# Sixteen meta queries and one filler product moved inside the first attention of a two-block kernel

## The chip, the cores and the metric

The kernel runs on one core of one Trainium2 chip. The metric is the device time of one execution in microseconds (us); the time before is the median of three runs. TensorE (PE) does the matrix products, VectorE (DVE) and ScalarE (ACT) the elementwise work, SyncE (SP) issues nearly all DMAs. Each engine runs its own instructions in a fixed order and waits on semaphores for the others.

## The reference, cut to what matters

The reference is two transformer blocks behind one another. The first one puts 16 meta tokens ahead of 512 tokens, normalises, projects, and mixes a state-space branch (`y_ssm`) with a differential attention branch. For each of 4 heads and each of 528 queries the attention is

```python
s = q . k                                  # two of them per head, j = 0 and 1
s = s - slope * dist ; s = where(dist >= 0, s, NEG_INF)
p = softmax(s)
w = p[:, :, 0] - lam * p[:, :, 1]
o = w @ v
y_att = rmsnorm(o, subln_g) * (1 - lam_init)
mixed = sigmoid(g_ssm) * (y_ssm @ w_ssm_out) + sigmoid(g_att) * (y_att @ w_att_out)
```

Then come an output product, a gated feed-forward part, and the second block (linear attention, sparse attention and two mixtures of experts). Only the first block's attention is touched by the change. Of the 16 meta queries only the last 2 are needed, for the convolution of the feed-forward part; the keys and values of all 16 are needed.

## The kernel before, in words

All large products are made of three float32 matmuls on split operands (`mm3`, lines 394 to 396: high by high, high by low, low by high). A weight tile is split into its high and low half by an ACT cast and a DVE subtraction (`split`, line 369). `dense_fm` makes one 128-row block of an output out of such matmuls; for 512 features in it issues 4 x 2 x 3 = 24.

The attention goes through 16 tiles, j = 0 to 15: query block i = j // 4 of 128 queries, head h = j % 4. I call them heads 0 to 15. `score` (lines 854 to 876) makes the two score tiles of a head on PE (line 861), adds the distance term (L863), takes the maximum (L867), the exponential on ACT (L869), the reciprocals (L870) and weighs the two halves into one (L874, L875). `weigh` (lines 878 to 895) transposes the weights on PE (L883), copies them back with ACT (L884 to L888), multiplies by the values (L893, tile `pv`), copies the result (DVE, L894) and sums its squares (ACT, L895). The score of head j + 1 is issued ahead of the weights of head j. After the fourth head of a query block `att_out` (lines 838 to 851) normalises: `rsq` (lines 433 to 440) is a chain of eleven small DVE instructions with the first one at L841, each using the result of the one before; then a scaling by row (the next L360), four transposes (L847, tile `yat`), and the high and low half of the result (ACT L850, DVE L851).

So that PE has work while the softmax runs, twelve products of the state-space branch are kept as fillers, in this order: `glu` 0 to 3 (lines 902 to 912) and `ssm_out` 0 to 7 (lines 923 to 928; its gate is read by DMA, L917, and goes through ACT at L918 and DVE at L919 and L920). One of them, 24 matmuls, is issued before `weigh` in each tile with j % 4 not zero:

```python
        nx = score((j + 1) // 4, (j + 1) % 4) if j < 15 else None
        if j % 4:
            filler(1)
        weigh(i, h, w_, osb, ss4)
```

After the 16 tiles stand the 16 meta queries (lines 946 to 982): eight tiny score products, a softmax on 16 partitions (L360, L959 to L965), four transposes, four products with the values, four sums of squares (L981) and an `att_out` of their own. Behind them the product with `w_att_out` begins (lines 988 to 992). Its columns come in two halves of 258 and 256 tokens, and all of `y_att` in a half has to be there for it.

The program is written in this order, but the order of the instructions on each engine is set before the run by a scheduler that looks at dependencies; what it made of the text is shown below where the prediction needs it.

Of the kernel before, what the change touches and what calls it, by code (L numbers as in the profile page):

```python
# [14 lines left out]
AF = mybir.ActivationFunctionType  # L15
ALU = mybir.AluOpType
AX = mybir.AxisListType
PSUM = bass.MemoryType.PSUM

P = 128  # L20
# [8 lines left out]
MID0 = T - MID  # L29
# [239 lines left out]
def build(ctx, tc, I, out, dbg=None):  # L269
    nc = tc.nc  # L270
    V, A, G, TE = nc.vector, nc.scalar, nc.gpsimd, nc.tensor
# [13 lines left out]
    def sb(n, tag, dt=F32, bufs=1):  # L285
        return ar.get(n, tag, dt, bufs)

    def p2(name):
        return pp_.tile([P, 2, 512], F32, tag="p2", name=name, bufs=3)
# [7 lines left out]
    def small(name, shape, dt=F32, bufs=1, tag=None):  # L297
        return sm.tile([P] + list(shape), dt, tag=tag or name, name=name, bufs=bufs)
# [60 lines left out]
    def tt(o, a, b, op, eng=None):  # L359
        return (eng or V).tensor_tensor(o, a, b, op=op)  # L360

    def bc(ap, n):
        return ap.unsqueeze(ap.ndim).to_broadcast(list(ap.shape) + [n])
# [83 lines left out]
    g1, ones, ident = (load_c(n, eng=nc.scalar) for n in ('g1', 'c_ones', 'c_ident'))  # L447
# [4 lines left out]
    with tc.manual_schedule(engines={mybir.EngineType.SP}):  # L452
# [5 lines left out]
        blk, b16 = load_c('c_blk'), load_c('c_b16')  # L458
# [253 lines left out]
    uT, qn = tiles(4, T, "uT"), tiles(4, T, "qn")  # L712
    for m in range(4):
        ps = dense_fm(KD, x1, HC)
# [27 lines left out]
    def filler(n):  # L742
        for _ in range(min(n, len(fill))):
            f, m = fill.pop(0)
            f(m)
# [18 lines left out]
    rq = small("rq", (40,))  # L764
# [21 lines left out]
    for c, (k0, n) in enumerate(kch):  # L786
        V.tensor_scalar(kdst[c], o[c][:n], r1c[:n, c:c + 1], None, op0=ALU.mult)
        s_ = sb(512, "t1", bufs=3)
# [49 lines left out]
    def att_out(osb, ss4, n, t0, skip=0):  # L838

        o4 = osb[:n].rearrange("p (h e) -> p h e", h=4)  # L840
        V.tensor_scalar(ss4[:n], ss4[:n], 1.0 / P, EPS, op0=ALU.mult, op1=ALU.add)  # L841
        r4 = small("r4", (4,), bufs=2)
        rsq(r4, ss4, (4,))
        tt(o4, o4, bc(r4[:n], P), ALU.mult)
        ps = p1("yat")
        for h in range(4):
            TE.transpose(ps[:, h * P:h * P + n], osb[:n, h * P:(h + 1) * P], ident[:n, :n])  # L847
        src = ps.rearrange("p (h t) -> p h t", h=4)[:, :, skip:n]
        hs = yahv[:, :, t0:t0 + n - skip]
        A.activation(hs, src, AF.Identity, scale=sgs)  # L850
        V.scalar_tensor_tensor(yalv[:, :, t0:t0 + n - skip], src, sgs, hs.bitcast(F32), op0=ALU.mult, op1=ALU.subtract)  # L851

    def score(i, h):
        n, q0 = NM + P * (i + 1), NM + P * i
        nb, w = (2, n // 2) if n > 512 else (1, n)
        pj, rj = [], []
        for j in range(2):
            ps = p2("sc")
            rows = slice(64 * j, 64 * j + 64)
            for b_ in range(nb):  # L860
                TE.matmul(ps[:, b_, :w], qn[h][rows, q0:q0 + P], knv[rows, h, b_ * w:(b_ + 1) * w], start=True, stop=True)
            s_ = sb(T, "s", bufs=6)
            V.scalar_tensor_tensor(s_[:, :n].rearrange("p (a b) -> p a b", a=nb), ps[:, :nb, :w],  # L863
                                   rq[:, 8 * (i + 1) + 2 * h + j:8 * (i + 1) + 2 * h + j + 1],
                                   dh[h][:, T - n:].rearrange("p (a b) -> p a b", a=nb), op0=ALU.mult, op1=ALU.add)
            mx = small("mx", (1,), bufs=6)
            V.tensor_reduce(mx, s_[:, :n], axis=AX.X, op=ALU.max, negate=True)  # L867
            se = small("se", (1,), bufs=6)
            A.activation(s_[:, :n], s_[:, :n], AF.Exp, bias=mx, accum_out=se)  # L869
            V.reciprocal(se, se)  # L870
            pj.append(s_)
            rj.append(se)
        tt(rj[1], rj[1], nlam, ALU.mult)
        V.tensor_scalar(pj[1][:, :n], pj[1][:, :n], rj[1], None, op0=ALU.mult)  # L874
        V.scalar_tensor_tensor(pj[0][:, :n], pj[0][:, :n], rj[0], pj[1][:, :n], op0=ALU.mult, op1=ALU.add)  # L875
        return pj[0]
# [53 lines left out]
    glu_b2 = small("glu_b2", (4,))  # L930
    V.tensor_scalar(glu_b2, glu_b, 0.5, None, op0=ALU.mult)
    fill = [(glu, m) for m in range(4)] + [(ssm_out, m) for m in range(8)]
    w_ = score(0, 0)
    for j in range(16):
        i, h = j // 4, j % 4
        if h == 0:
            osb = sb(512, "osb", bufs=2)
            ss4 = small("ss4", (4,), bufs=2)
        nx = score((j + 1) // 4, (j + 1) % 4) if j < 15 else None
        if j % 4:  # L940
            filler(1)
        weigh(i, h, w_, osb, ss4)
        w_ = nx
        if h == 3:
            att_out(osb, ss4, P, 2 + P * i)
    ps = p2("sc16")
    for h in range(4):
        for j in range(2):
            rows = slice(64 * j, 64 * j + 64)
            TE.matmul(ps[:16, j, (h * 16):(h + 1) * 16], qn[h][rows, 0:16], knv[rows, h, 0:16], start=True, stop=True)  # L950
    s_ = sb(256, "s", bufs=6)
    sv = s_[:16, :128].rearrange("p (h j k) -> p h j k", h=4, j=2)
    rq0 = rq[:16, 0:8].rearrange("p (h j) -> p h j", j=2)
    for j in range(2):
        tt(sv[:, :, j], ps[:16, j, :64].rearrange("p (h k) -> p h k", h=4), bc(rq0[:, :, j], 16), ALU.mult)
    s3 = s_[:16, :128].rearrange("p (a k) -> p a k", k=16)
    tt(s_[:16, :128], s_[:16, :128], b16, ALU.add)
    mx = small("mx8", (8,))[:16]
    V.tensor_reduce(mx, s3, axis=AX.X, op=ALU.max)  # L959
    tt(s3, s3, bc(mx, 16), ALU.subtract)  # L960
    A.activation(s_[:16, :128], s_[:16, :128], AF.Exp)
    V.tensor_reduce(mx, s3, axis=AX.X, op=ALU.add)
    V.reciprocal(mx, mx)
    m2 = mx.rearrange("p (h j) -> p h j", j=2)
    V.tensor_scalar(m2[:, :, 1], m2[:, :, 1], nlam[:16], None, op0=ALU.mult)  # L965
    tt(s3, s3, bc(mx, 16), ALU.mult)
    w16 = s_[:16, 128:192]
    tt(w16.rearrange("p (h k) -> p h k", h=4), sv[:, :, 0], sv[:, :, 1], ALU.add)
    ps = p2("w16t")
    for h in range(4):  # L970
        TE.transpose(ps[:16, 0, h * 16:(h + 1) * 16], w16[:, h * 16:(h + 1) * 16], ident[:16, :16])
    w16t = s_[:16, 192:256]
    A.copy(w16t, ps[:16, 0, :64])
    for h in range(4):
        TE.matmul(ps[:16, 1, h * P:(h + 1) * P], w16t[:, h * 16:(h + 1) * 16], vm[:, h * P:(h + 1) * P], start=True, stop=True)
    osb = sb(512, "osb", bufs=2)
    ss4 = small("ss4", (4,), bufs=2)
    V.memset(ss4, 1.0)
    A.copy(osb[:16], ps[:16, 1])
    for h in range(4):  # L980
        A.activation(ps[:16, 0, h * P:(h + 1) * P], osb[:16, h * P:(h + 1) * P], AF.Square, accum_out=ss4[:16, h:h + 1])  # L981
    att_out(osb, ss4, 16, 0, skip=MID0)
    drop_tiles("qn", "dh", "uT", "zh", "zl")
    drop("kn", "vt", "vm", "s", "wT", "osb")
    ya = pairs([yahv[:, h] for h in range(4)], [yalv[:, h] for h in range(4)])
# [29 lines left out]
    ps = p2("rs2")  # L1015
# [997 lines left out]
```

## Time and profile before

| | |
|---|---|
| median of three runs | 1919.12 us (1915.56 to 1922.62) |
| the profiled execution | 1922.88 us, span of its records 1921.1 us |
| PE busy with matmuls | 1749.1 us (91%), 10719 instructions |
| DVE busy | 1219.8 us (63%) |
| ACT busy | 877.3 us (46%) |
| mean granted TensorE clock | 0.948 of full speed |

Times of the trace count from the start of the span. The first attention with its fillers lies between about 255 and 374 us. "Busy" of PE is the time in which some matmul is in its pipeline. An idle time in brackets stands before the instruction that ended it, with the instruction that released it behind the arrow. SBUF tiles are cut from pages and are all called `pg`; PSUM tiles keep their names (`sc`, `wtp`, `pv`, `yat`, `mm`).

### The profile page before, as it was taken

How to read it: one execution, taken by the hardware profiler on the slowest of the kernel's cores; microseconds unless marked ns; L12 is line 12 of the kernel's file. 1: busy time of each engine (PE TensorE's matmuls, PEld its weight loads, DVE VectorE, ACT ScalarE, POOL GpSimd, SP SyncE). 2: the span in 40 equal slices, each digit the busy share in tenths (PEclk: the TensorE clock that was granted, in tenths of full speed). 3: DMA queues.
4: the chain of work that ended last, by engine and by line, in shares of the span. 5: the costliest groups of instructions: out<-in, count | busy, mean ns of one | idle time of the engine just before them, and what ended most of it. 6: DMA issues, size and time to landing. Idle time of an engine off the chain costs nothing.

```text
span 1921.1 us, 27208 instructions
## 1 busy us (share of the span) xinstructions
PE 1749.1 (91%) x10719; PEld 1484.6 (77%) x10719; DVE 1219.8 (63%) x2276; ACT 877.3 (46%) x1397; POOL 168.2 (9%) x140
## 2 busy tenths in 40 slices
PE   8999999899999999999999699949998999869990
PEld 7899877798989988877888578838786777648870
DVE  7755368776555543235347879874437777678985
ACT  4233346433333332234213278854235675638881
POOL 2310000022000000000000112110000000012213
PEclk9999999899999999999989899979899999979995
DMA  5435222242222233222215589762131003548953
GB/s 194 111 109 139 89 88 65 64 158 96 103 89 88 92 140 106 94 88 88 88 67 203 185 292 382 300 230 77 58 140 45 1 12 111 203 156 327 382 216 140
DMA packets 69206, 269.73 MB, mean 140 GB/s; under 512 B 22144, under 2 KB 24721, under 8 KB 44241
## 3 DMA queue, kind: packets, MB, share of 16 engines
q1 hardware_dynamic: 52384, 246.38, 36.0%
q0 software_dynamic: 9216, 16.80, 2.3%
q10 hardware_dynamic: 7472, 4.76, 1.2%
q8 instruction: 85, 1.39, 0.3%
q14 instruction: 49, 0.39, 0.1%
HBM read 249.62 MB, written 30.43 MB: 146 GB/s over the span
## 4 chain that ended last, share of the span: by engine, by line
PE 64%; DVE 6%; ACT 3%; DMA 2%; issue 1%; POOL 0%; POOLq 0%; SPq 0%; DVEq 0%; ACTq 0%
PE mm L396 8%; PE mm L395 8%; PE mm L394 8%; PE psh L395 3%; PE psh L396 3%; PE psh L394 3%; PE tm L395 2%; PE tm L394 2%; PE tm L396 2%; PE npo L1932 2%; PE npt L1920 2%; PE op L395 2%; PE op L394 2%; PE op L396 2%; PE xgt L1436 1%
## 5 line engine op out<-in xcount | busy, mean ns | idle before, releaser
L369 ACT CAST pg<-pg 128x1024 fp32r<-128x1024 f32 (+2 forms) x437 | 428.3, 1003 | 564.3 <-PE mm L395 225.3
L369 DVE TENSOR_TENSOR pg<-pg,pg 128x1024 fp32r<-128x1024 f32 (+2 forms) x437 | 503.3, 1175 | 277.5 <-ACT pg L369 262.6
L396 PE MATMUL mm<-pg,pg 128*128 128x258 f32 (+2 forms) x1504 | 483.3, 322 | 3.9 <-DVE pg L369 3.8
L394 PE MATMUL mm<-pg,pg 128*128 128x258 f32 (+2 forms) x1504 | 485.3, 323 | 1.4 <-ACT pg L888 0.7
L395 PE MATMUL mm<-pg,pg 128*128 128x258 f32 (+2 forms) x1504 | 482.9, 321 | 0.0
L394 PEld LDWEIGHTS mm<-pg,pg 128*128 128x128 f32 x1504 | 288.0, 192 | 27.8 <-ACT pg L886 2.7
L396 PEld LDWEIGHTS mm<-pg,pg 128*128 128x128 f32 x1504 | 287.0, 191 | 25.0 <-DVE pg L369 4.7
L395 PEld LDWEIGHTS mm<-pg,pg 128*128 128x128 f32 x1504 | 287.9, 191 | 21.2 <-issue 0.4
L360 DVE TENSOR_TENSOR pg<-mm,pg 128x256 f32<-128x256 f32 (+3 forms) x138 | 66.3, 510 | 140.2 <-PE mm L396 140.2
L394 PE MATMUL psh<-pg,pg 128*128 128x512 f32 x256 | 106.3, 415 | 7.4 <-ACT pg L369 7.4
L395 PE MATMUL psh<-pg,pg 128*128 128x512 f32 x256 | 106.0, 414 | 1.3 <-DVE pg L369 1.3
L396 PE MATMUL psh<-pg,pg 128*128 128x512 f32 x256 | 104.3, 407 | 0.7 <-DVE pg L369 0.6
L395 PE MATMUL tm<-pg,pg 128*128 128x512 f32 x192 | 76.9, 401 | 2.2 <-DVE pg L369 2.2
L396 PE MATMUL tm<-pg,pg 128*128 128x512 f32 x192 | 76.0, 396 | 0.0
L394 PE MATMUL tm<-pg,pg 128*128 128x512 f32 x192 | 75.5, 403 | 0.0
L360 DVE TENSOR_TENSOR pg<-pg,pg 128x512 f32<-128x512 f32 (+12 forms) x103 | 57.6, 580 | 24.9 <-ACT pg L675 9.3
L1904 ACT ACTIVATE pg<-ns,nmx 128x512 f32<-128x512 f32 (+3 forms) x128 | 66.5, 535 | 11.3 <-DVE nmx L1900 7.2
L394 PEld LDWEIGHTS psh<-pg,pg 128*128 128x128 f32 x256 | 50.2, 196 | 19.0 <-ACT pg L369 8.7
L1900 DVE TENSOR_REDUCE nmx<-ns 128x2 f32<-128x1024 f32 (+3 forms) x48 | 50.0, 1042 | 17.0 <-PE ns L1897 16.8
L360 DVE TENSOR_TENSOR pg<-pg 128x64 f32<-128x64 f32 (+8 forms) x127 | 49.3, 409 | 17.4 <-ACT pg L1033 15.4
L1426 POOL DMA_INDIRECT pg<-xd,idx x32 | 39.5, 1236 | 236.4 <-DVE wts L360 128.0
L395 PEld LDWEIGHTS psh<-pg,pg 128*128 128x128 f32 x256 | 50.2, 196 | 12.9 <-DVE pg L369 2.5
(440 smaller groups left out, 2955.0 us busy)
## 6 DMA issues: line engine op xcount, KB each, us to landing
pg<-in_w_moe_dram SPq DMA_DIRECT2D x96, 1024.0 KB
pg<-in_w_up_dram SPq DMA_DIRECT2D x22, 1024.0 KB
pg<-in_w_dn_dram SPq DMA_DIRECT2D x11, 1024.0 KB
pg<-in_w_g_dram SPq DMA_DIRECT2D x8, 1024.0 KB
pg<-in_w_go_dram SPq DMA_DIRECT2D x8, 1024.0 KB
pg<-yd SPq DMA_DIRECT2D x16, 512.0 KB
pg<-in_w_n_dram SPq DMA_DIRECT2D x8, 1024.0 KB
pg<-in_w_no_dram SPq DMA_DIRECT2D x8, 1024.0 KB
```

The lines of the kernel that those rows point to most:

```text
L360: return (eng or V).tensor_tensor(o, a, b, op=op)
L369: return A.copy(h, src), V.tensor_tensor(l, src, h.bitcast(F32), op=ALU.subtract)
L394: TE.matmul(o, a[0], b[0], start=start, stop=False)
L395: TE.matmul(o, a[0], b[1], start=False, stop=False)
L396: return TE.matmul(o, a[1], b[0], start=False, stop=stop)
L1426: ld = G.indirect_dma_start(out=xg, out_offset=None, in_=self.xd, in_offset=bass.IndirectOffsetOnAxis(ap=self.idx[:, e:e + 1], axis=0), bo ...
L1436: i = TE.transpose(ps[:, k // 4, (k % 4) * P:(k % 4 + 1) * P], xg[:, k * P:(k + 1) * P], ident)
L1900: V.tensor_reduce(mx, sc, axis=AX.X, op=ALU.max, negate=True)
L1904: A.activation(pp[:, r, br], sc[:, r, br], AF.Exp, bias=mx[:, r, br:br + 1], accum_out=se[:, r, br:br + 1])
L1920: TE.transpose(src[:, r, br, c * P:(c + 1) * P], pp[:, r, br, c * P:(c + 1) * P], ident)
L1932: TE.matmul(o_[64 * r:64 * r + 64], vsw[:, c * 512 + br * 256 + g * 64:c * 512 + br * 256 + (g + 1) * 64], pts[r][:, br, c * P:(c + 1) * P ...
```

## The change

The meta queries become a function `meta()`, called after the weights of head 8; its tiles `osb16` and `ss16` are those of `att_out` for it. The filler call of tile j = 1 is dropped; the fillers keep their order, so that each of the first eleven comes in the next tile that has one, and the twelfth is issued after the weights of head 15, ahead of the last `att_out`. No arithmetic changes.

```diff
+    def meta():
+
+        ps = p2("sc16")
...
+        w16 = s_[:16, 128:192]
...
+        osb16 = sb(512, "osb", bufs=2)
+        ss16 = small("ss16", (4,))
+        V.memset(ss16, 1.0)
+        A.copy(osb16[:16], ps[:16, 1])
...
+        att_out(osb16, ss16, 16, 0, skip=MID0)
+
     w_ = score(0, 0)
     for j in range(16):
         i, h = j // 4, j % 4
@@ -937,49 +977,16 @@
             osb = sb(512, "osb", bufs=2)
             ss4 = small("ss4", (4,), bufs=2)
         nx = score((j + 1) // 4, (j + 1) % 4) if j < 15 else None
-        if j % 4:
+        if j % 4 and j > 1:
             filler(1)
         weigh(i, h, w_, osb, ss4)
         w_ = nx
+        if j == 8:
+            meta()
+        if j == 15:
+            filler(1)
         if h == 3:
             att_out(osb, ss4, P, 2 + P * i)
-    ps = p2("sc16")
...
-    att_out(osb, ss4, 16, 0, skip=MID0)
```

What the scheduler makes of it shows at three places. At the start, on PE, around the scores of heads 2 and 3 (`sc`), the transposes of head 1 (`wtp`) and the first filler (`mm`); the rows with + are new here, the filler's first two matmuls follow them:

```order
 L893 MATMUL pv<-pg_243,pg_81 128x128
 L861 MATMUL sc<-pg_80,pg_428 128x144
+L883 MATMUL wtp<-c_ident,pg_132 16x128
+L883 MATMUL wtp<-c_ident,pg_132 128x128
+L861 MATMUL sc<-pg_80,pg_428 128x144 x2
+L893 MATMUL pv<-pg_102,pg_2687 128x128
+L893 MATMUL pv<-pg_243,pg_2687 128x128
 L394 MATMUL mm<-pg_2622,pg_430 128x258
 L395 MATMUL mm<-pg_2623,pg_430 128x258
```

The filler stood behind the second row and now stands behind the value products of head 1.

In the middle, on DVE, ahead of the first score row of head 11 (the L863). Before (a row of the normaliser of query block 1, head 10's weights, then the score):

```order
L440 SCALAR_TENSOR_TENSOR r_3111<-rsqt,r_3111 128x4
L875 SCALAR_TENSOR_TENSOR pg_132<-pg_132,se,pg_81 128x400
L360 TENSOR_TENSOR rsqt<-r_3111 128x4
L863 SCALAR_TENSOR_TENSOR pg_81<-sc,rq,pg_262 128x400
L439 SCALAR_TENSOR_TENSOR rsqt<-rsqt,ss_2889 128x4
```

With the change (`ss_3166` and `r_3174` are the meta queries' sums and factors, `pg_430` a weight tile):

```order
L440 SCALAR_TENSOR_TENSOR r_3174<-rsqt,r_3174 128x4
L360 TENSOR_TENSOR rsqt<-r_3174 128x4
L439 SCALAR_TENSOR_TENSOR rsqt<-rsqt,ss_3166 128x4
L440 SCALAR_TENSOR_TENSOR r_3174<-rsqt,r_3174 128x4
L360 TENSOR_TENSOR pg_2687<-pg_2687,r_3174 16x512
L919 SCALAR_TENSOR_TENSOR pg_3062<-pg_3062,mm 128x258
L920 SCALAR_TENSOR_TENSOR pg_3062<-pg_3062,mm 128x256
L369 TENSOR_TENSOR pg_430<-pg_92,pg_430 128x1024
L863 SCALAR_TENSOR_TENSOR pg_2687<-sc,rq,pg_262 128x400
```

Head 10's weights lie well ahead now, and the whole chain of the meta normaliser, which nothing interleaves, has come in between them and head 11's score.

At the end, on PE, from the last value products (`pv`, here of head 15) to the product with `w_att_out` (`mm<-pg_2620`, `mm<-pg_2621`). Before:

```order
L893 MATMUL pv<-pg_102,pg_2687 128x128
L893 MATMUL pv<-pg_243,pg_2687 128x128 x4
L971 MATMUL w16t<-c_ident,pg_132 16x16 x4
L975 MATMUL w16t<-pg_102,pg_132 16x128 x4
L847 MATMUL yat<-c_ident,pg_2687 128x128 x4
L847 MATMUL yat<-c_ident,pg_132 128x16 x4
L394 MATMUL mm<-pg_2620,pg_430 128x258 x2
```

With the change (the first row is the last matmul of the twelfth filler):

```order
L396 MATMUL mm<-pg_2624,pg_483 128x256
L893 MATMUL pv<-pg_243,pg_2687 128x128 x4
L394 MATMUL mm<-pg_2620,pg_430 128x258
L395 MATMUL mm<-pg_2621,pg_430 128x258
L396 MATMUL mm<-pg_2620,pg_430 128x258
L394 MATMUL mm<-pg_2620,pg_430 128x258
L395 MATMUL mm<-pg_2621,pg_430 128x258
L396 MATMUL mm<-pg_2620,pg_430 128x258
L394 MATMUL mm<-pg_2620,pg_483 128x258
L395 MATMUL mm<-pg_2621,pg_483 128x258
L396 MATMUL mm<-pg_2620,pg_483 128x258
L847 MATMUL yat<-c_ident,pg_132 128x128 x4
```

The meta products are gone from here, and nine matmuls on the first column half of the next product have come ahead of the last transposes.

## Rows read from the trace of the kernel before

**Rows 1.** Stages: us; busy PE, PEld, DVE, ACT, POOL; granted clock, DMA share, GB/s
```profile
274.54:287.90 13.36, 11.83 (x75) 9.24 (x74) 9.13 (x31) 9.65 (x29) 0.00 (x0) 1.00 0.47 159
287.90:315.91 28.01, 26.39 (x163) 19.94 (x163) 25.27 (x77) 17.93 (x57) 0.00 (x0) 1.00 0.16 50
315.91:324.76 8.85, 6.96 (x47) 5.10 (x47) 8.20 (x31) 5.57 (x18) 0.00 (x0) 1.00 0.13 35
324.76:349.24 24.48, 22.20 (x146) 18.79 (x147) 20.40 (x53) 15.68 (x40) 0.00 (x0) 0.93 0.23 71
349.24:374.16 24.92, 18.43 (x152) 15.62 (x152) 19.62 (x68) 12.99 (x41) 0.00 (x0) 0.90 0.30 97
374.16:379.25 5.09, 5.09 (x23) 5.09 (x24) 0.20 (x1) 0.00 (x0) 0.00 (x0) 0.50 0.18 52
344.50:347.40 2.90, 2.90 (x24) 2.90 (x24) 2.90 (x12) 2.31 (x7) 0.00 (x0) 1.00 0.00 0
```

**Rows 2.** Timeline, PE at the end: start us, us, instruction, [idle before, releaser]
```profile
360.75 4.55 PE L893 MATMUL pv<-pg,pg 16*128 16x128 f32 x30 [0.45 <-DVE pg L851]
369.05 1.01 PE L847 MATMUL yat<-c_ident,pg 128*128 128x128 f32 x4 [1.78 <-DVE pg L360]
373.22 0.58 PE L847 MATMUL yat<-c_ident,pg 16*128 16x16 f32 x4 [3.16 <-DVE pg L360]
```

**Rows 3.** Timeline, DVE at the end: meta softmax, normaliser, scaling, low halves
```profile
360.52 0.33 DVE L360 TENSOR_TENSOR pg<-sc,rq 16x64 f32<-16x64 f32 x2
364.60 0.21 DVE L360 TENSOR_TENSOR pg<-pg 16x64 f32<-16x64 f32 x1
366.12 0.17 DVE L841 TENSOR_SCALAR ss<-ss 128x4 f32<-128x4 f32 x1 [0.49 <-ACT pv L895]
368.30 0.69 DVE L360 TENSOR_TENSOR pg<-pg,r 128x512 f32<-128x512 f32 x1
371.35 0.74 DVE L851 SCALAR_TENSOR_TENSOR pg<-yat,sgs,pg 128x512 fp32r<-128x512 f32 x1
374.14 0.23 DVE L851 SCALAR_TENSOR_TENSOR pg<-yat,sgs,pg 128x8 fp32r<-128x8 f32 x1 [1.07 <-ACT pg L850]
```

**Rows 4.** Timeline, ACT at the end: the meta queries' copy, a square, the high half
```profile
367.36 0.58 ACT L979 COPY pg<-w16t 16x512 f32<-16x512 f32 x1 [0.65 <-PE w16t L975]
368.40 0.27 ACT L981 ACTIVATE w16t<-pg 16x128 f32<-16x128 f32 x1
368.62 0.18 ACT L981 ACTIVATION_READ_ACCUMULATOR w16t<-pg 16x1 f32 x1
370.09 0.69 ACT L850 ACTIVATE pg<-yat,sgs 128x512 fp32r<-128x512 f32 x1 [0.43 <-PE yat L847]
```

**Rows 5.** Timeline, start: scores, a gate on ACT, head 1's transposes, a filler's DVE pass
```profile
277.36 0.51 PE L861 MATMUL sc<-pg,pg 64*128 64x144 f32 x2
279.58 0.64 ACT L918 ACTIVATE pg<-pg 128x514 f32<-128x514 f32 x1 [0.86 <-DMA pg<-sgd]
281.42 0.38 PE L883 MATMUL wtp<-c_ident,pg 128*16 128x128 f32 x2 [0.49 <-DVE pg L875]
283.00 0.69 DVE L910 SCALAR_TENSOR_TENSOR pg<-pg,pg 128x514 f32<-128x514 f32 x1
```

**Rows 6.** Timeline, middle, DVE and ACT: a split, a head's two weighing passes, an exponential
```profile
314.41 1.22 DVE L369 TENSOR_TENSOR pg<-pg,pg 128x1024 fp32r<-128x1024 f32 x1
320.99 0.42 DVE L874 TENSOR_SCALAR pg<-pg,se 128x400 f32<-128x400 f32 x1
322.49 0.62 DVE L875 SCALAR_TENSOR_TENSOR pg<-pg,se,pg 128x400 f32<-128x400 f32 x1
327.14 0.61 ACT L869 ACTIVATE pg<-pg,mx 128x400 f32<-128x400 f32 x1
```

**Rows 7.** Timeline, PE: the two longest waits between the start and the last tiles
```profile
323.26 0.60 PE L883 MATMUL wtp<-c_ident,pg 128*16 128x128 f32 x4 [1.62 <-DVE se L360]
349.24 0.70 PE L883 MATMUL wtp<-c_ident,pg 128*16 128x128 f32 x5 [1.62 <-DVE se L870]
```

More of the change, by code (lines that the diff above doesn't have):

```diff
@@ L932, in build @@
     fill = [(glu, m) for m in range(4)] + [(ssm_out, m) for m in range(8)]
+    def meta():
+        ps = p2("sc16")
+        for h in range(4):
+            for j in range(2):
+                rows = slice(64 * j, 64 * j + 64)
+                TE.matmul(ps[:16, j, (h * 16):(h + 1) * 16], qn[h][rows, 0:16], knv[rows, h, 0:16], start=True, stop=True)
+        s_ = sb(256, "s", bufs=6)
+        sv = s_[:16, :128].rearrange("p (h j k) -> p h j k", h=4, j=2)
+        rq0 = rq[:16, 0:8].rearrange("p (h j) -> p h j", j=2)
+        for j in range(2):
+            tt(sv[:, :, j], ps[:16, j, :64].rearrange("p (h k) -> p h k", h=4), bc(rq0[:, :, j], 16), ALU.mult)
+        s3 = s_[:16, :128].rearrange("p (a k) -> p a k", k=16)
+        tt(s_[:16, :128], s_[:16, :128], b16, ALU.add)
+        mx = small("mx8", (8,))[:16]
+        V.tensor_reduce(mx, s3, axis=AX.X, op=ALU.max)
+        tt(s3, s3, bc(mx, 16), ALU.subtract)
+        A.activation(s_[:16, :128], s_[:16, :128], AF.Exp)
+        V.tensor_reduce(mx, s3, axis=AX.X, op=ALU.add)
+        V.reciprocal(mx, mx)
+        m2 = mx.rearrange("p (h j) -> p h j", j=2)
+        V.tensor_scalar(m2[:, :, 1], m2[:, :, 1], nlam[:16], None, op0=ALU.mult)
+        tt(s3, s3, bc(mx, 16), ALU.mult)
+        w16 = s_[:16, 128:192]
+        tt(w16.rearrange("p (h k) -> p h k", h=4), sv[:, :, 0], sv[:, :, 1], ALU.add)
+        ps = p2("w16t")
+        for h in range(4):
+            TE.transpose(ps[:16, 0, h * 16:(h + 1) * 16], w16[:, h * 16:(h + 1) * 16], ident[:16, :16])
+        w16t = s_[:16, 192:256]
+        A.copy(w16t, ps[:16, 0, :64])
+        for h in range(4):
+            TE.matmul(ps[:16, 1, h * P:(h + 1) * P], w16t[:, h * 16:(h + 1) * 16], vm[:, h * P:(h + 1) * P], start=True, stop=True)
+        osb16 = sb(512, "osb", bufs=2)
+        ss16 = small("ss16", (4,))
+        V.memset(ss16, 1.0)
+        A.copy(osb16[:16], ps[:16, 1])
+        for h in range(4):
+            A.activation(ps[:16, 0, h * P:(h + 1) * P], osb16[:16, h * P:(h + 1) * P], AF.Square, accum_out=ss16[:16, h:h + 1])
+        att_out(osb16, ss16, 16, 0, skip=MID0)
     w_ = score(0, 0)
@@ L943, in build @@
         w_ = nx
+        if j == 8:
+            meta()
+        if j == 15:
+            filler(1)
         if h == 3:
             att_out(osb, ss4, P, 2 + P * i)
-    ps = p2("sc16")
[L947 to L981, printed above, removed]
-    att_out(osb, ss4, 16, 0, skip=MID0)
     drop_tiles("qn", "dh", "uT", "zh", "zl")
```

## The prediction

> **What bounds the kernel now.** I read the page first (table above): PE is the busiest engine over the whole span, so a change inside the attention is worth what it does to PE's idle time there, not to any engine's sum. Then I cut the attention into five stages with the view of engines by stretch [rows 1], at instants that can be found again in the changed kernel: the first score row on DVE (L863) of heads 4, 9 and 11, the transposes of head 13's weights (L883), and the first matmul of the product with `w_att_out` behind the last `yat`. I call them A to E; they last 13.36, 28.01, 8.85, 24.48 and 24.92 us. The reader should see that DVE is nearly as full as PE: in stage B 25.27 us of DVE stand beside 26.39 of PE, in stage C 8.20 us of 8.85 are DVE's and only 6.96 are PE's. So the softmax on DVE sets the pace in C, and both engines together in B and D. Only E has room on both (18.43 and 19.62 of 24.92).
>
> Then the timeline of PE at the end [rows 2]: the value products of the last three heads end at 365.30 (360.75 + 4.55), and the next product begins at 374.16. In between PE idles 1.78 us for the normaliser of query block 3, 3.16 us for that of the meta queries, and the clock falls: the stretch after it runs 23 matmuls in 5.09 us at a granted clock of 0.50, where 24 take 2.90 us at 1.00 [rows 1]. That is the lower of the two levels, 1.2 GHz, after some 9 us of scattered small products; it costs 2.3 us. This gap is what the change fills. The question is what it pays elsewhere.
>
> **The change, stage by stage.** The order of each engine (shown with the change) gives what moves; durations are from rows.
>
> *A, the first filler gone.* 24 matmuls (2.90 us) and two DVE passes of 0.69 us [rows 1, 5] leave the stage. PE did not need the room: its queue waited at 281.42 for head 1's weights, which waited for an exponential behind a gate on ACT that came by DMA at 279.58 [rows 5]. This wait stays, now with PE empty from the end of the scores at 277.87 on, 3.5 us [rows 5]. DVE saves 1.37 us of passes, so the stage could end 1.3 us sooner. But the filler now follows the transposes of head 1 and two more scores (281.42 + 0.38 + 2 x 0.51, an estimate of 282.8), and head 2's transposes queue behind it on PE. If the clock has fallen in the gap, the filler loses what the lower level cost stage D, 7% of 24.48 us or 1.7 us [rows 1], and the stage ends by as much later. The 3.5 us without work are more than the 1.62 us before the transposes at 323.26 [rows 7], which ended with that lower clock; so I take the lower level: **+0.4 us**, ends -1.3 and +1.0.
>
> *B, each filler one place later.* PE's load stays. DVE loses a split (1.22) and the two passes of a head's weights (0.42 + 0.62) that fall into C, and gains the two passes from A (1.37) [rows 5, 6]: -0.9 us. PE and DVE share this stage, so I take half: **-0.5**, ends 0 and -0.9.
>
> *C, the meta queries.* DVE has no room, so its queue is what I add up. The meta softmax is ten instructions of 0.2 to 0.3 us, 2.3 us together (first and last in [rows 3]). The meta normaliser is eleven instructions that start 0.20 us apart because each needs the last (366.12 to 368.30 for the same chain), then 0.69 to scale and 0.23 for the low half [rows 3]: 3.1 us, with nothing of another head between them. The scheduler draws other work ahead of head 11's score: the split and a head's weights of above (2.3), and scaling and low half of query block 1 (0.69 + 0.74) [rows 3, 6]: 3.7 us. Waits are new, since head 10 now stands alone: both reciprocals wait for their exponentials (0.61 us, and a read-out as long as that of a square, 0.18) [rows 4, 6] with only one or no DVE instruction to cover them: 0.45 and 1.0 us by hand. Before the meta normaliser ACT has a high half (0.69), the copy (0.58) and five sums of squares (0.45 each) [rows 4], 3.5 us, against 2.4 us of DVE work: 1.1 us. Head 10's score waits 0.3 us for the meta transposes ahead of it on PE. That is 2.85 us of waits, against 0.65 us that DVE idled in C before [rows 1]. Sum: 2.3 + 3.1 + 3.7 + 2.2 = **+11.3 us**, ends +8.5 (no waits) and +12.5. On PE the small meta products lie within this, covered.
>
> *D gives a part back.* Query block 1's scaling and low half (1.43) have left DVE. PE, fuller here (22.20 of 24.48, DVE 20.40), has one value product of a head less (about 1.2 us, a third of 4.55 for the shorter block) [rows 1, 2], and its first filler starts some 1.3 us ahead of head 11's score instead of level with it. Stage D also lost its 1.7 us to the lower clock level [rows 1]. If the clock holds, all of it goes: **-4.0**, ends -1.4 (DVE's part alone) and -5.5 (down to DVE's remaining work). The Trainium skill, page TensorE: Matmul & The Clock Gate, section HAM oscillation, says that waits between bursts of matmuls make the next burst start throttled each time. Rows 7 agree by half: two waits of 1.62 us, the clock of D fell after the first, but the 24 matmuls after 349.24 ran at pitch. By the page D would keep its 1.7 us, and the whole sum would be 8.0.
>
> *E, the end.* Up to the end of head 15's value products the stage took 16.06 us (349.24 to 365.30) [rows 2, 7]. It gains one filler (2.90) and loses the wait at 360.75 (0.45) and the meta scores ahead of it (taken as long again): 18.1. From there to the next product it was 5.5 us for query block 3 alone (365.30 to 370.09 + 0.69) [rows 2, 4]; the rest to 374.16 was the meta queries and falls away. But on DVE a split (1.22) [rows 6] stands between the filler's passes and the copy of head 15's values, and it can begin only when the last filler has finished with the old weights: +1.5 with hand-offs, 7.0. E is then 25.1 us, +0.2 on before, and nine matmuls of the next product (1.1 us) are already done in it: **-0.9**, ends -2.3 (the split not in the way) and +0.5. PE still idles over 4 us before the last transposes, so I leave the lower clock after it as it is: 0, or -2.3 if it holds.
>
> Sum: 0.4 - 0.5 + 11.3 - 4.0 - 0.9 = **+6.3 us** for the profiled execution, 1922.88 to 1929.2. That execution lies 3.76 above the median of the runs, so the forecast is **1925.4 us**. What lies behind the attention keeps its order but for a few neighbours, and is priced at 0. About 0.5% (9.6 us) is what a measurement of this kernel can tell from no change; 6.3 is within it. The forecast spans +3 to +9.5.
>
> **Rivals.** *The cover works as written.* DVE idles 11.7 us in A to D (74.70 less 63.00 busy) [rows 1], more than the 5.4 of the meta queries. If those fit in, C and D together cost nothing, A ends 1.3 sooner, B 0.5, the split is not in the way in E (-2.3) and the clock holds behind it (-2.3): -6.4, **1912.7 us**. For it speaks the gap at the end; against it that C itself has 0.65 us of DVE idle time, and that the chain stands unbroken in DVE's order. Chance 0.15; in a third of it the gain passes 0.5%.
>
> *Half cover.* C takes its work without waits (11.3 - 2.2 = 9.1), D falls to DVE's floor (-5.5), the split is hidden (-2.3): +1.2, **1920.3 us**. Chance 0.20.
>
> *Slower, by PE left waiting in C.* PE has the old 6.96 us of work [rows 1] and the small meta products in a C of 20 us, so it stands still for half of it. If it is throttled there, the first filler of D runs at the lower level (+1.7) and D gives back DVE's 1.4 alone; with A at +1.0 that is 1.0 - 0.5 + 11.3 + 0.3 - 0.9 = +11.2, **1930.3 us**. It decides from the point where D gives back less than about 0.7 us. The Trainium skill, TensorE: Matmul & The Clock Gate, HAM oscillation, speaks for it. Against it: one of the two waits in rows 7 left the clock alone, and the first filler of C runs while DVE is still in its chain. Chance 0.17, nearly all beyond 0.5%.
>
> That the change does nothing is excluded by the orders.
>
> **How the numbers follow.** Forecast 0.48, all within 0.5%. Faster by over 0.5%: 0.05 (of the cover). Slower: 0.14 (of the throttled C). The rest, 0.48 + 0.20 + 0.10 + 0.03 = 0.81, is no change that can be told. The range reaches from 1914, which leaves out the better part of the cover, to 1932, a little above the throttled C. The bounds of the stages, taken all to one side, give -3.8 and +12.6, or 1915.3 and 1931.7, which lie inside it.
>
> **What would show it.** Right: head 4's score within 1.3 us of before; C, from head 9's to head 11's first score row, 19 to 21 us long with the meta normaliser's rows 0.20 us apart on DVE and nothing of another head in them; D near 20 us; the wait of the last `yat` for L360 still 4 us or more, with the copy L894 of head 15 behind an L369. Wrong: C under 16 us (DVE found the room), a first matmul after the last `yat` at full pitch, or a D of 23 us or more with a clock under 0.9. A difference of over 3 us behind the attention would break the zero that I put there.

## The result, and the profile after

The changed kernel takes **1931.53 us** (median of 5 runs, 1929.83 to 1934.35) against 1919.18 for the kernel before on the same chip: 1.0056 times as long, 95% interval 1.0039 to 1.0073. Measured once more on another chip it was 1932.30 against 1923.18, 1.0051 (1.0031 to 1.0072). So it is slower by 9 to 12 us, about half a per cent, where the forecast was +6.3 and 1925.4 us. Its profiled execution took 1931.53 us with a span of 1929.8 (+8.7).

The engines by stage, cut at the same instants as in [rows 1] (the attention starts at 273.25 here, 1.29 us earlier than before, since the stretch ahead of it happened to be shorter):

```profile
273.25:287.92 14.67, 11.34 (x51) 8.68 (x50) 8.11 (x30) 8.42 (x28) 0.00 (x0) 0.65 0.41 144
287.92:315.10 27.18, 25.36 (x161) 19.39 (x162) 24.14 (x74) 17.45 (x56) 0.00 (x0) 1.00 0.12 39
315.10:337.01 21.91, 16.50 (x92) 11.79 (x92) 16.74 (x61) 10.06 (x33) 0.00 (x0) 0.69 0.05 13
337.01:359.85 22.84, 19.53 (x135) 16.25 (x134) 18.72 (x52) 13.07 (x37) 0.00 (x0) 1.00 0.26 81
359.85:385.57 25.72, 21.63 (x152) 19.11 (x152) 15.54 (x44) 12.54 (x32) 0.00 (x0) 0.93 0.33 104
385.57:390.66 5.09, 5.09 (x31) 5.02 (x32) 1.37 (x3) 0.00 (x0) 0.00 (x0) 0.70 0.19 52
```

Against [rows 1] this is A +1.31, B -0.83, C +13.06, D -1.64, E +0.80: +12.70 up to the product with `w_att_out`. That product makes some up: from its first matmul behind the last transposes to the last row of L998 on DVE (L991 before) it takes 24.42 us instead of 27.71, because nine matmuls are done ahead and the clock is back sooner (31 matmuls in 5.09 us at 0.70, before 23 at 0.50). What follows is +0.6. The sum, -1.29 + 12.70 - 3.29 + 0.6, is the +8.7 of the span.

C is the place. The timeline of PE there (the fillers' rows left out):

```profile
317.78 0.60 PE L883 MATMUL wtp<-c_ident,pg 128*16 128x128 f32 x4 [0.80 <-DVE pg L875]
318.30 0.37 PE L939 MATMUL sc<-pg,pg 64*16 64x16 f32 x16
323.29 0.26 PE L960 MATMUL w16t<-c_ident,pg 16*16 16x16 f32 x4 [4.62 <-DVE pg L360]
323.48 1.71 PE L861 MATMUL sc<-pg,pg 64*128 64x400 f32 x4
327.97 2.37 PE L893 MATMUL pv<-pg,pg 16*128 16x128 f32 x8
```

The tiny transposes of the meta weights (L960) stand in PE's queue ahead of head 10's scores (L861) and wait 4.62 us for the meta softmax; the scores, which need nothing of it, wait behind them. Then everything runs at the lower clock level (granted 0.50 from 322 to 334): the eight value products take 2.37 us here and 1.35 in D. DVE in the same stretch:

```profile
319.24 0.17 DVE L841 TENSOR_SCALAR ss<-ss 128x4 f32<-128x4 f32 x1 [0.86 <-ACT pv L895]
325.22 0.63 DVE L863 SCALAR_TENSOR_TENSOR pg<-sc,rq,pg 128x400 f32<-128x400 f32 x1 [1.47 <-PE sc L861]
328.66 0.16 DVE L870 RECIPROCAL se<-se 128x1 f32<-128x1 f32 x1 [0.79 <-ACT pg L869]
331.72 0.16 DVE L841 TENSOR_SCALAR ss<-ss 16x4 f32<-16x4 f32 x1 [0.72 <-ACT w16t L970]
331.92 0.17 DVE L435 TENSOR_SCALAR r<-ss 128x4 int32<-128x4 int32 x1
333.70 0.16 DVE L440 SCALAR_TENSOR_TENSOR r<-rsqt,r 128x4 f32<-128x4 f32 x1
333.89 0.68 DVE L360 TENSOR_TENSOR pg<-pg,r 16x512 f32<-16x512 f32 x1
```

The meta normaliser runs alone, from 331.72 to 333.89 in steps of 0.20 us, as foretold. DVE is busy 16.74 us and idle 5.17, of which the four waits shown make 3.84; the prediction had counted 2.85 us of waits in all.

At the end, PE and DVE answer to [rows 2] and [rows 3]:

```profile
384.14 0.66 PE L847 MATMUL yat<-c_ident,pg 128*128 128x128 f32 x4 [3.17 <-DVE pg L360]
385.57 1.01 PE L394 MATMUL mm<-pg,pg 128*128 128x256 f32 x3 [0.78 <-ACT pg L850]
```

```profile
379.30 1.22 DVE L369 TENSOR_TENSOR pg<-pg,pg 128x1024 fp32r<-128x1024 f32 x1
380.44 0.28 DVE L894 COPY pg<-pv 128x128 f32<-128x128 f32 x1
383.39 0.69 DVE L360 TENSOR_TENSOR pg<-pg,r 128x512 f32<-128x512 f32 x1
```

One wait of PE is left there instead of two, but the split of the last filler (L369) stands ahead of the copy of head 15's values.

### The profile page after: what moved, and what is told of

Its sections match the earlier page's. It is cut to its first block, busy times and chain, and to the rows that moved or that the text cites. A ratio compares the mean times of both kernels' runs of the same rounds, so it can differ in the third digit from the quotient of the medians.

```text
span 1929.8 us, 27200 instructions
## 1 busy us (share of the span) xinstructions
PE 1754.5 (91%) x10719; PEld 1488.7 (77%) x10719; DVE 1221.2 (63%) x2276; ACT 876.9 (45%) x1397; POOL 166.7 (9%) x140
## 4 chain that ended last, share of the span: by engine, by line
PE 80%; DVE 9%; ACT 4%; DMA 3%; issue 2%; ACTq 0%; POOL 0%; POOLq 0%; SPq 0%; DVEq 0%
PE mm L394 11%; PE mm L395 11%; PE mm L396 11%; PE psh L396 3%; PE psh L395 3%; PE psh L394 3%; DVE pg L360 3%; PE npo L1939 2%; PE tm L395 2%; PE tm L394 2%; PE tm L396 2%; PE npt L1927 2%; PE op L395 2%; PE op L394 2%; PE op L396 2%
## 5 line engine op out<-in xcount | busy, mean ns | idle before, releaser
L369 ACT CAST pg<-pg 128x1024 fp32r<-128x1024 f32 (+2 forms) x437 | 428.1, 1003 | 564.6 <-PE mm L395 225.1
L369 DVE TENSOR_TENSOR pg<-pg,pg 128x1024 fp32r<-128x1024 f32 (+2 forms) x437 | 504.0, 1177 | 275.7 <-ACT pg L369 260.7
```

The costliest lines, as they stand in the source:

```text
L369: return A.copy(h, src), V.tensor_tensor(l, src, h.bitcast(F32), op=ALU.subtract)
```

## The experiments

**How they are read.** Beside each median stand three lengths from the profiled execution: *middle*, from the transposes of head 8's weights to those of head 13's (the end of B, C and D); *E*, from there to the first matmul of the product with `w_att_out` behind the last transposes; *attention*, from the transposes of head 0's weights to that same matmul. "Before" and "changed" are the two kernels of this study.

| kernel | median us | ratio to before (95%) | middle | E | attention |
|---|---|---|---|---|---|
| before | 1919.18, 1922.56, 1923.18, 1923.54 | | 32.47 | 24.92 | 99.18 |
| changed | 1931.53 | 1.0056 (1.0039 to 1.0073) | 42.07 | 25.72 | 111.88 |
| e5 changed again | 1932.30 | 1.0051 (1.0031 to 1.0072) | 42.41 | 25.72 | 112.86 |
| e1 meta alone | 1927.09 | 1.0021 (1.0001 to 1.0041) | 41.04 | 23.20 | 106.78 |
| e2 fillers alone | 1933.02 | 1.0066 (1.0046 to 1.0087) | 30.42 | 31.77 | 106.84 |
| e3 meta after head 14 | 1935.63 | 1.0062 (1.0038 to 1.0085) | 30.35 | 35.48 | 109.86 |
| e4 meta after head 15 | 1918.63 | 0.9976 (0.9952 to 1.0000) | 30.92 | 24.72 | 99.03 |
| e12 the same again | 1915.75 | 0.9962 (0.9937 to 0.9988) | 31.02 | 25.01 | 98.58 |
| e6 meta in two parts | 1927.01 | 1.0021 (1.0004 to 1.0038) | 36.06 | 25.18 | 106.02 |
| e7 a filler in the wait | 1928.23 | 1.0036 (1.0019 to 1.0054) | 37.99 | 25.74 | 108.15 |
| e8 no meta | 1920.85 | 0.9987 (0.9970 to 1.0004) | 30.19 | 24.69 | 100.03 |
| e9 two parts, fillers as before | 1921.15 | 0.9973 (0.9950 to 0.9995) | 40.14 | 22.04 | 109.10 |
| e10 two parts, short chain | 1927.29 | 1.0011 (0.9990 to 1.0033) | 36.89 | 25.79 | 108.18 |
| e11 last filler in the gap | 1918.36 | 0.9974 (0.9950 to 0.9998) | 31.06 | 27.23 | 100.84 |

e1 to e4 ran on one chip, e5 to e8 on another, e9 to e12 on a third; the four medians of before belong to the first measurement and to these three.

A caution: from that product to the end the profiled executions took 1539.9 to 1549.5 us, and two executions of one kernel differ there by 3.9 (changed) and 6.0 us (e4 and e12), while their attention differs by 1.0 and 0.5. So the trace of the attention tells causes better than a single whole time, and a median tells prices to some 4 us. The whole time goes with the granted clock: among the runs of one kernel those with a higher mean clock are shorter (before, on the third chip: 1910.78 us at 0.955, 1937.17 at 0.939). An estimate by a line through the 95 runs of before in the three later measurements: 1.6 us for each thousandth. The trace of the attention has its share too: the middle of before is 32.47 us at a clock of 0.95, and 30.92 to 31.06 at 1.00 in e4, e11 and e12, which have the same work there.

**e1 and e2: one half of the change each.** e1 is the changed kernel with the fillers of before; e2 the one with the meta queries behind all tiles.

```diff
 e1, against the changed kernel:
-        if j % 4 and j > 1:
+        if j % 4:
...
-        if j == 15:
-            filler(1)
 e2, against the changed kernel:
-        if j == 8:
-            meta()
...
             att_out(osb, ss4, P, 2 + P * i)
+    meta()
```

> The meta queries after the weights of head 8 as in the change, the fillers where they were before. Theory (the meta queries' place is what costs): stage C is 20 to 23 us long as with the change (21.91), the tail behind the last query block is some 3 us shorter than before because its own meta part is gone, and the first and last stages keep the filler of tile 1; in sum 1926 to 1930 us, most of the +12. Rival (the shift of the fillers is what costs, with an empty first stage and a split ahead of the last copy): 1919 us or less, as fast as before.

> The fillers as in the change (none in tile 1, the twelfth after the weights of head 15), the meta queries after all tiles as before. Theory: stage A is 1 to 1.5 us longer (filler at the lower clock), stage C stays at 8 to 10 us, the end is a little longer because the split of the twelfth filler stands ahead of the copy of head 15's values: 1919 to 1923 us. Rival (the fillers carry the loss): 1926 us or more. Other rival (the filler covers the gap at the end, the clock holds): under 1916 us.

e1 measured +4.5 us on before, e2 +10.5 (by the ratios 4.0 and 12.7). The theory was half wrong: the middle of e1 is as long as with the change (41.04), but the fillers' shift carries a loss too, and alone a larger one. e2's PE at the end shows why:

```profile
370.43 0.26 PE L960 MATMUL w16t<-c_ident,pg 16*16 16x16 f32 x4 [3.96 <-DVE rsqt L439]
378.88 0.57 PE L847 MATMUL yat<-c_ident,pg 16*128 16x16 f32 x4 [4.89 <-DVE pg L360]
```

In the kernel before, the meta scores stood ahead of 30 value products [rows 2], which covered the softmax: PE waited 0.74 us ahead of the meta products, and not at all for the meta weights:

```profile
365.23 0.26 PE L971 MATMUL w16t<-c_ident,pg 16*16 16x16 f32 x4
366.23 1.04 PE L975 MATMUL w16t<-pg,pg 16*16 16x128 f32 x8 [0.74 <-ACT pg L973]
```

In e2 the twelfth filler and the value products come first, the meta scores last, and the softmax, the products and the normaliser run one after the other in the open: 3.96 and 4.89 us of PE's time, E 31.77 us. And the filler taken from tile 1 bought nothing: of its 2.90 us of PE and two passes of DVE nothing has come off the attention at the transposes of head 13 (75.07 us from those of head 0; 74.26 before, 74.31 in e4).

Taken together, e1 against the changed kernel gives the fillers' price where the meta queries are not at the end: E 25.72 instead of 23.20 (+2.5), attention +5.1 (111.88) or +6.1 (112.86).

**e3 and e4: the meta queries at other places.** e3 is the changed kernel with the call after head 14; e4 is the kernel before with the meta queries ahead of the last normalisation instead of behind it.

```diff
 e3, against the changed kernel:
-        if j == 8:
+        if j == 14:
             meta()
 e4, against the changed kernel:
-        if j % 4 and j > 1:
+        if j % 4:
...
-        if j == 8:
+        if j == 15:
             meta()
-        if j == 15:
-            filler(1)
```

> The changed kernel with the call of the meta queries moved from after head 8 to after head 14; fillers as in the change. In the last stage DVE is busy 15.7 of 25.7 us while PE has fillers to run, so the meta chain should fit there. Theory (DVE's room at the place of the call decides): stage C back at 9 to 10 us, last stage 0 to 3 us longer than with the change, 1917 to 1923 us. Rival (the chain costs its own length wherever it stands): 1927 us or more.

> The kernel before with the meta queries called after the weights of head 15 and ahead of the last normalisation instead of behind it, so that the two normaliser chains alternate on DVE; fillers as before. Theory: an instruction of a lone chain takes 0.20 us because it waits for the one before, two chains together take little longer than one, so the end is 2 to 3.5 us shorter: 1915.5 to 1917.5 us. Rival (the meta softmax delays the copy and the sums of the last query block by as much as is saved): within 1 us of before.

e3 is as slow as the change, though its middle is back at 30.35 us: the rival was right. PE at its end:

```profile
365.08 0.25 PE L960 MATMUL w16t<-c_ident,pg 16*16 16x16 f32 x4 [2.38 <-DVE pg L360]
377.47 0.53 PE L847 MATMUL yat<-c_ident,pg 16*128 16x16 f32 x4 [3.94 <-DVE pg L360]
384.40 1.09 PE L847 MATMUL yat<-c_ident,pg 128*128 128x128 f32 x4 [1.85 <-DVE pg L360]
```

DVE had room, and it did not help: the first two stand in PE's queue ahead of a filler and of head 15's value products, and the last transposes follow them. So the room of another engine alone does not decide.

In e4 the two normaliser chains alternate. Its DVE (a row of x2 is one instruction of each chain):

```profile
363.39 0.17 DVE L841 TENSOR_SCALAR ss<-ss 128x4 f32<-128x4 f32 x1 [0.49 <-ACT pv L895]
366.97 0.16 DVE L841 TENSOR_SCALAR ss<-ss 16x4 f32<-16x4 f32 x1 [3.41 <-ACT w16t L970]
367.16 0.24 DVE L435 TENSOR_SCALAR r<-ss 128x4 int32<-128x4 int32 x2
368.93 0.24 DVE L440 SCALAR_TENSOR_TENSOR r<-rsqt,r 128x4 f32<-128x4 f32 x2
369.13 1.28 DVE L360 TENSOR_TENSOR pg<-pg,r 16x512 f32<-16x512 f32 x2
```

Ten steps of both chains take 1.97 us (367.16 to 369.13), as long as those of one. That part of the theory holds. But query block 3's chain, ready at 363.4, now waits 3.41 us for the meta squares, so E is only 0.2 us shorter. The time fell by 3.9 us (4.6 by the ratio, interval up to 0), and in a second measurement, e12, by 7.8:

> The kernel with the meta queries ahead of the last normalisation once more. Its first measurement gave 4.6 us below the kernel before, with an interval up to 0, but its trace from the first head's weights to the product behind the attention is as long as before within 0.2 us. By the trace: within 2 us of before. By the first measurement: 3 to 6 us below.

So this version is, by the intervals, 0.1 to 0.6% faster than before in e12, beyond both expectations; its attention accounts for 0.2 to 0.6 us of it. The rest goes with the clock: the twelve runs of e12 had a mean granted clock of 0.951, the 35 of before beside them 0.947, and by the estimate above 4.4 thousandths are 7 us. Whether the order of this kernel brings the higher clock, or chance did, stays open.

**e5 to e8: what the middle costs.** e5 is the changed kernel again. e6 cuts `meta()` in two, e7 puts a filler in front of the meta transposes, e8 leaves the meta queries out.

```diff
 e6, against the changed kernel:
+        return s_, w16
+
+    def meta2(s_, w16):
         ps = p2("w16t")
...
         if j == 8:
-            meta()
+            held = meta()
+        if j == 9:
+            meta2(*held)
 e7, against the changed kernel:
+        filler(1)
         ps = p2("w16t")
...
-        if j % 4 and j > 1:
+        if j % 4 and j not in (1, 9):
 e8, against the changed kernel:
+    V.memset(yahv[:, :, 0:2].bitcast(F32), 0.0)
+    V.memset(yalv[:, :, 0:2].bitcast(F32), 0.0)
...
-        if j == 8:
-            meta()
```

> The changed kernel itself, for comparison with the next three on the same chip. Expected from its first measurement, ratio 1.0056: 9 to 13 us above the kernel before. The first four runs gave the meta queries alone +4.5 us and the fillers alone +10.5; if the two add up it would be +15, and by the theory that the fillers' loss in the second of these was the meta softmax left uncovered at the end, which the change does not have, it is +9 to +13.

> The changed kernel with the meta queries in two parts: scores and softmax after head 8, transposes and all behind them after head 9. The scores of the next head then do not stand behind the meta transposes on PE. Theory (PE standing still for 4.6 us in stage C, and the lower clock after it, is part of the price): the stretch from the weights of head 8 to those of head 13 is 2 to 4 us shorter than with the change, the time 2 to 4 us lower, and the clock in it stays at 1.00. Rival (the length of DVE's queue sets stage C, PE's wait is covered): within 1 us of the changed kernel.

> The changed kernel with the filler of tile 9 issued inside the meta queries, between their scores and their transposes, so that PE works for 2.9 us of the 4.6 that it waited; the order of the scores behind the transposes stays. Theory (lower clock): clock of stage C near 1.00 instead of 0.69, 1.5 to 3 us below the changed kernel. Rival (DVE's queue): the same time within 1 us, or up to 2 us more, because the filler's passes and its split (2.0 us) now stand in DVE's meta chain.

> The changed kernel without the meta queries' scores, softmax, values and normalisation; their two columns are set to zero. It gives the whole price of the meta queries at head 8. Theory: stages C and D together are back at 31 to 33 us, 8 to 10 us below the changed kernel, so 1 to 3 us above the kernel before in spite of the work left out, because the twelfth filler at the end costs 2.8 us and the one taken from the start gave nothing. Rival (the filler shift alone would pay if the meta queries cost nothing): at least 3 us below the kernel before.

Against e5 on the same chip: e6 -5.3 us, e7 -4.1, e8 -11.5, each more than expected. In the middle stretch, by the view of engines, the change, then e8, e6, e7:

```profile
317.78:359.85 42.07, 34.14 (x217) 27.01 (x218) 32.78 (x106) 22.19 (x66) 0.00 (x0) 0.84 0.14 44
```

```profile
318.78:348.97 30.19, 27.13 (x186) 22.02 (x186) 27.41 (x84) 19.72 (x54) 0.00 (x0) 1.00 0.19 61
```

```profile
319.89:355.95 36.06, 33.08 (x217) 26.09 (x218) 31.25 (x105) 20.59 (x63) 0.00 (x0) 0.86 0.18 52
```

```profile
320.88:358.87 37.99, 32.45 (x217) 25.55 (x218) 32.39 (x107) 22.82 (x66) 0.00 (x0) 0.91 0.16 49
```

The meta queries at head 8 cost the change 12 us (42.07 or 42.41 against 30.19). In e6 6.0 to 6.4 of them are gone: with the next scores ahead of the meta transposes PE's wait is 1.17 us instead of 4.62, and the middle falls to 36.06. Two more things differ. The meta normaliser does not stand alone before head 11's score any more, but among the score rows of head 12. And the clock, which was expected to hold, fell at another place: it was 0.50 from 320 to 326 and 1.00 from 328 to 350, behind the meta transposes, where the change has 0.50 from 322 to 334; the eight value products took 1.35 us there, and 2.37 in the change. How much of the 6 us each of the three has cost is not told apart, and e9 below warns against giving all of it to the order on PE. With a filler in the wait (e7) 4.1 to 4.4 us come off, though DVE's work is much the same (32.39 us, with the change 32.78): DVE's queue alone does not set this stage. The clock is a rival here too, 0.91 over the stretch against 0.84.

e6's PE at the meta transposes:

```profile
320.83 0.40 PE L939 MATMUL sc<-pg,pg 64*16 64x16 f32 x16
321.17 2.90 PE L861 MATMUL sc<-pg,pg 64*128 64x400 f32 x4
329.86 0.25 PE L964 MATMUL w16t<-c_ident,pg 16*16 16x16 f32 x4 [1.17 <-DVE pg L360]
```

e8 answers the other question, between its theory and its rival: even with the meta queries costing nothing the filler shift does not pay to speak of, 2.3 us below before (interval from 5.8 below to 0.8 above) although the kernel before lets PE wait 3.16 us for them at its end [rows 2]. Its E is as long as before (24.69), with the twelfth filler where the meta queries were.

**e9 to e11.** e9 is e6 with the fillers of before; e10 is e6 with a meta normaliser of two instructions instead of eleven; e11 is e4 with the last filler behind the meta queries.

```diff
 e9, against e6:
-        if j % 4 and j > 1:
+        if j % 4:
...
-        if j == 15:
-            filler(1)
 e10, against e6:
-        rsq(r4, ss4, (4,))
+        rsq(r4, ss4, (4,), 0 if skip else 3)
...
-        for _ in range(3):
+        for _ in range(steps):
 e11, against e4:
-        if j % 4:
+        if j % 4 and j < 15:
...
             meta()
+            filler(1)
```

> The meta queries in two parts as in the run before (softmax after head 8, transposes and the rest after head 9), and the fillers where they were in the kernel before. Theory (three prices add: PE's stand behind the meta transposes 5 to 6 us, DVE's meta work 5 to 6, the filler shift 3 to 5): without the first and the third, 1 us below to 3 us above the kernel before. Rival (the filler shift costs nothing by itself): as the split with the change's fillers, +4 or more.

> The meta queries in two parts with the fillers of the change, and the meta normaliser without its nine correction instructions (the two meta columns are then normalised by the first estimate alone). Theory (with PE's stand gone, DVE's queue sets the pace, and each instruction of the lone chain costs its 0.20 us): 1.5 to 2.2 us below the split with the full chain, so about +2 us on the kernel before. Rival (the chain is covered once PE does not stand): within 0.7 us of the split.

> The kernel with the meta queries ahead of the last normalisation (fillers as before but for one): the filler of tile 15 is issued behind the meta queries, so that it runs in the gap in which DVE waits 3.4 us for the meta squares and PE 5.4 us for the normalisation. Theory: the weights of head 15 come 2.9 us earlier, the meta products 2.1 later behind the filler: 0.5 to 2 us below the same kernel without this move. Rival (the filler's split and passes push the normalisers back by their 2.0 us): 1 to 2 us above it.

e9 came out 2.4 us below before by the medians (5.2 by the ratio), somewhat below what the theory gave, and with a mean clock of 0.950 in its runs against 0.947 of before; but its trace shows an attention of 109.10 us, 9.9 longer than before, in an execution that was the slowest of its runs (1925.67). The two do not fit together, so the adding up of the three prices is not shown. The trace also bears on e6. Here too the scores of head 10 stand ahead of the meta transposes, and PE waits 1.40 us for them:

```profile
322.68 1.87 PE L861 MATMUL sc<-pg,pg 64*128 64x400 f32 x4
331.21 0.26 PE L964 MATMUL w16t<-c_ident,pg 16*16 16x16 f32 x4 [1.40 <-DVE rsqt L439]
```

Yet the middle is 40.14 us, only 0.9 less than in e1, which has the same fillers and these scores behind the transposes. Behind these transposes the clock was 0.50 from 331 to 341, and the meta normaliser ran alone again (339.67 to 341.84). So in this execution the order on PE by itself gave next to nothing; by the medians, each against before on its own chip, e9 is 6.9 us below e1. The whole times speak for the split, this trace does not.

e10 has a chain shorter by 1.8 us, yet its middle is not shorter (36.89 against 36.06); its ratio is 0.1% lower, within both intervals. But the clock differs again: behind the meta transposes it was 0.50 from 332 to 336 in e10 and 1.00 in e6, the filler there took 4.8 us (333.62 to 338.38) instead of 2.9 (333.57 to 336.51), and DVE waited for it:

```profile
338.58 0.42 DVE L919 SCALAR_TENSOR_TENSOR pg<-pg,mm 128x258 f32<-128x258 f32 x1 [2.83 <-PE mm L396]
```

So the trace speaks neither for the theory, that each instruction of the chain is paid in full once PE does not stand, nor against it.

e11 is 2.6 us above e12 on the same chip, and its attention 2.3 us longer: the rival's sign, by another way. The weights of head 15 came only 0.4 us earlier (83.19 us after those of head 0, 83.61 in e12), not 2.9: with the filler gone PE waited 1.66 us for DVE's normaliser of query block 2 instead, so much of the filler was covered where it stood before. PE's wait at the end stayed (5.75 us). Both waits:

```profile
353.41 0.65 PE L847 MATMUL yat<-c_ident,pg 128*128 128x128 f32 x4 [1.66 <-DVE pg L360]
372.31 1.63 PE L847 MATMUL yat<-c_ident,pg 16*128 16x16 f32 x8 [5.75 <-DVE pg L360]
```

## Why the prediction was right, and where it was not

It forecast a loss too small to tell at +6.3 us with ends 1914 and 1932; it became +9 to +12, at the edge of the 9.6 us that it took for what can be told, and inside the range; both intervals lie wholly above 1. The profiled executions give +8.7, or +10.0 without the 1.29 us by which the attention happened to start earlier. The forecast lies 6.1 us under the measured median; some 3.5 us of that may be the base, since the kernel before had medians of 1922.56 to 1923.54 later, over 29 to 35 runs, against the 1919.12 of three runs that the sum started from. Not shown: on its own chip the change was 12.35 us above before. Of the rivals the two covers were wrong, and the slower one (1930.3) is nearest in time, PE's standing still in C included, but not in what it said of D. By its steps:

**A (+0.4, ends -1.3 and +1.0): +1.31.** The mechanism was right: PE empty (2.64 us ahead of head 1's transposes), the clock at 0.50, the filler 24 matmuls in 4.9 us (282.08 to 287.01) instead of 2.9. The size was above the upper end. It comes again: with the filler gone from tile 1 the transposes of head 2 come 12.73 to 13.84 us after those of head 0 in all eight profiled executions, with it at 11.85 to 12.64 in five of six (the sixth is e9, 15.63, with the clock at 0.50 from 285 to 289). **B (-0.5): -0.83**, inside.

**C (+11.3, ends 8.5 and 12.5): +13.06,** above the upper end. DVE's added work was summed at 9.1 us and is 8.54. The term that failed is "Head 10's score waits 0.3 us for the meta transposes ahead of it on PE": DVE waited 1.47 us there, and PE 4.62. I had seen the order and priced the transposes, not the wait that they carry for everything behind them. All waits were put 2.2 us above before; DVE's idle time grew by 4.5 (5.17 against 0.65). And the reason given for the stage, "DVE has no room, so its queue is what I add up", was only part of it: e7 takes away 4 us with as much work on DVE, and e6 6 us, there with the meta normaliser moved on as well. What the lower clock cost in C, which the sum left out, is not told apart.

**D (-4.0, ends -1.4 and -5.5): -1.64.** "If the clock holds, all of it goes" failed: the clock held at 1.00 over the whole stage, and 1.64 us came back. The rival "PE left waiting in C" foresaw a small return, but through a lower clock in D; that is not what happened. ACT was held by a gate still to come by DMA, with the exponential behind it, and PE and DVE waited for each other by turns:

```profile
339.62 0.64 ACT L918 ACTIVATE pg<-pg 128x514 f32<-128x514 f32 x1 [2.58 <-DMA pg<-sgd]
```

```profile
340.89 0.17 DVE L870 RECIPROCAL se<-se 128x1 f32<-128x1 f32 x1 [1.43 <-ACT pg L869]
348.29 0.42 DVE L919 SCALAR_TENSOR_TENSOR pg<-pg,mm 128x258 f32<-128x258 f32 x1 [1.74 <-PE mm L396]
```

```profile
359.85 0.71 PE L883 MATMUL wtp<-c_ident,pg 128*16 128x128 f32 x5 [2.36 <-DVE rsqt L360]
```

2.7 us less of PE's work and 1.7 less of DVE's gave 1.64 less time; neither engine was full all through (19.53 and 18.72 us of 22.84).

**E (-0.9 with the nine early matmuls; length +0.2): length +0.80, and -3.29 in the product behind.** The split ahead of the copy was right. The lower clock was not expected in E itself (0.50 at 362 to 364, after the wait of 2.36 us above), and behind E it ended sooner than I took it.

Of what was to be seen, the chain in steps of 0.20 us with nothing of another head and the copy behind an L369 came true; C at 19 to 21 us (21.91), D near 20 (22.84) and a last wait of 4 us (3.17) did not; head 4's score, 1.31 us later into the attention, is at the limit that was set. Of the signs that would have made it wrong none appeared, though the time behind the attention, 2.7 us shorter with the product, came near the 3 us that were set.

The steps are off by +0.9, -0.3, +1.8, +2.4 and, for E with the product behind it, -1.6 us. That the sum is off by only 2.4 us in the profiled executions is in part luck: the sooner return of the clock behind E, which was not foreseen, and the earlier start take back 2.9 of the 4.1 us that C and D missed.

That the change would not pay rested on a right reason (work put into a stage whose engines depend on each other at every head). The experiments add one that was not seen: the filler shift has a price of its own. The prediction took the filler out of A as worth something in part and the twelfth filler as filling a gap. Nothing came off in front, since PE waits there for other things, and E grew by 2.5 us (e1 against the changed kernel).

## What to carry to other kernels

On an engine that runs its queue in order, a small instruction that waits on a long chain costs the wait of everything behind it: put its consumers behind the next ready work, not directly behind its producer (e6: half of the price was gone, though not by the order alone, and e9's trace shows only 0.9 us). A filler is worth its length only where the engine would otherwise wait; taken from such a place it gives nothing back, and put at the end it pushes what was covered there into the open (e2). Two chains of small dependent instructions can run in the time of one (e4: ten steps of two chains in 1.97 us, as one); it pays only if the second does not make the first wait (there 3.41 us). And a clock that falls at another place can hide or imitate the effect under test (e9, e10): compare it before comparing lengths.

## What was not expected of the hardware

A wait of PE of the same length had both outcomes. Ahead of the transposes of head 13's weights PE waited 2.29 us in e2 and in e7. In e2 (transposes at 348.04) the granted clock stayed at 1.00 from 346 to 356; in e7 (at 358.87) it was 0.50 from 360 to 362 and 0.68 in the two us after. The Trainium skill, page TensorE: Matmul & The Clock Gate, section HAM oscillation, tells of a kernel whose waits between bursts make the next burst start throttled each time. The waits there were longer than these, a condition that the prediction left out; the two traces here agree with it once and once not, as [rows 7] did. What PE did before does not settle it: both profiled executions of the changed kernel waited 2.36 us at this place, and two us later the clock was 0.50 in the first (transposes at 359.85) and 1.00 in e5 (at 361.18):

```profile
362.00:364.00 2.00, 2.00 (x10) 2.00 (x11) 1.97 (x4) 0.69 (x2) 0.00 (x0) 0.50 0.00 0
362.00:364.00 2.00, 2.00 (x17) 1.61 (x17) 1.90 (x6) 1.12 (x4) 0.00 (x0) 1.00 0.47 133
```

And the time from the product behind the attention to the end, in which the order of the instructions is the same but for single neighbours, ranged over 9.6 us between profiled executions. The traces show what goes with it: by their clock records TensorE was at the lower level for 166 to 171 us of that time in the four shortest (1539.9 to 1541.2 us), and for 184 to 201 in those above 1546. Most of the difference between e4 and e12 arises at one place. There e4 falls back by 7.4 us, with these rows for e4 and e12:

```profile
995.00:1000.00 5.00, 5.00 (x26) 5.00 (x25) 2.55 (x11) 1.02 (x1) 0.95 (x1) 0.50 0.28 91
995.00:1000.00 5.00, 5.00 (x46) 5.00 (x46) 3.90 (x14) 1.03 (x1) 0.95 (x1) 1.00 0.34 106
```

PE had been busy without a gap in both since 985. Why the clock fell in one of them was not tried.
